# When the gMLP parameters are loaded, and into which buffers

## The chip, the cores and the metric

One core of one Trainium2 chip runs the whole block. The metric is the device time of one execution in microseconds. TensorE (PE) multiplies, VectorE (DVE) does the elementwise float work, ScalarE (ACT) copies, rounds and evaluates functions, GpSimd (POOL) helps out, and the queue of SyncE (SP) issues nearly all transfers from device memory.

## The reference, cut to what matters

The kernel computes one transformer-like layer on 512 tokens of width 1024: an adaptive norm, one wide input product, two mixers (HGRN2 and gMLP), gates, an output product and a SwiGLU network. The change is about the gMLP mixer:

```
v = gelu(zv);  v = layer_norm(v) * ln_w + ln_b
w = where(block_mask, w_s, 0)                 # 8 groups of 128 x 128
sv = einsum('gts,bnsgc->bntgc', w, v) + b_s   # over 4 blocks of 128 tokens
return gelu(zu) * sv
```

## The kernel before, in words

Every float32 operand of a large product is split in two: a high half, a rounded copy made by ScalarE ("whi", "uh", "mix"), and a low half, the remainder, made by VectorE ("wlo", "ul", "mix"). One product of 128 x 128 x 512 is then three matmuls. The split halves of the weights have two buffers each, so the split for one block can begin when TensorE is done with the block before the last.

The stage in question comes in this order on TensorE. First the last block of zu (256 columns). Then the 1024 x 1024 product zv, made with seven half-size products instead of eight (`zt7`, lines 579 to 620): seven factors in the order 1, 2, 5, 6, 7, 4, 3, of 24 matmuls each. Factors 1, 2 and 4 use quarters of the activations as they are; 5, 7, 6 and 3 use sums of quarters, made by `mixes` (lines 542 to 577): four sums "uq" of high and low halves, the difference "mixs", three further sums, and four splits into "mix". On the side of the weights, factors 5, 6, 7 and 4 use sums of two quarters of the weights, formed in place (line 191). The quarters are loaded as they come up: two into the rotating buffers "raw", two ("rawq", lines 170 to 178) into the pool ua.

After zv come the norm of gelu(zv) (`ln_fin`, `affine`), the gate product (`zw`, line 676), and between its pieces the spatial products (`spatial`, line 661), which need the transposed spatial weights "wT" and the bias "bsb".

Two pools matter. ua has twelve buffers of 8 KB per partition; at this time it holds the activations' halves uh and ul (two buffers each), and then the parameter tiles "glnp" and "bw", the six tiles of `mixes` and the two rawq. ub has five; gu takes two, gv two. A third pool has one buffer of the tag "s4", used by the staging tile "wst" of the spatial weights and by "mixs" in turn. A tile that gets a used buffer waits until the last reader of its former owner is done.

The instructions of TensorE and of the SP queue run in the order of the program. Those of VectorE, ScalarE and GpSimd are ordered beforehand by a planner, with the program's order as priority, and each engine then keeps that order. `keep_in_program_order` sets an instruction behind the one written before it on its engine. `later(n, fn)` calls fn after n ticks; a tick is half of a 128-column product, or half a factor. Four ticks pass in the last block of zu and two in each factor. `get` splits the next block one tick on, and issues the load of the block after it.

Before the change the parameters were loaded (lines 623 to 633) ahead of the last block of zu; `w_transpose` (line 635) stood between that block and `mixes`. It transposes the eight 128 x 128 matrices on TensorE into two PSUM banks, and VectorE copied them into wT, leaving out the masked corner.

Of the kernel before, what the change touches and what calls it, by code (L numbers as in the profile page):

```python
# [7 lines left out]
F32 = mybir.dt.float32  # L8
F32R = mybir.dt.float32r
U8 = mybir.dt.uint8  # L10
AF = mybir.ActivationFunctionType
OP = mybir.AluOpType
# [3 lines left out]
P = 128  # L16
T = 512
NT = T // P
D = 1024
# [12 lines left out]
def f32(ap):  # L32
    return ap.bitcast(F32)
# [17 lines left out]
def body(ctx, tc, x, c, w_ada, b_ada, w_in, b_gate, lb_logits, norm_w, w_proj_a, g_ln_w, g_ln_b,  # L51
# [3 lines left out]
    w_ada, b_ada, w_in, b_gate, norm_w = w_ada[0], b_ada[0], w_in[0], b_gate[0], norm_w[0]  # L55
    w_proj_a, g_ln_w, g_ln_b, g_ws, g_bs = w_proj_a[0], g_ln_w[0], g_ln_b[0], g_ws[0], g_bs[0]
# [3 lines left out]
    V, A, G, PE = nc.vector, nc.scalar, nc.gpsimd, nc.tensor  # L60
# [5 lines left out]
    ua = ctx.enter_context(tc.tile_pool(name="ua", bufs=12))  # L66
# [8 lines left out]
    def acc_ps():  # L75
        return acc.tile([P, 512], F32, name="acc")

    def side_ps():
        return side.tile([P, 512], F32, name="sps")

    def s2(name="s2"):
        return tmp["s2"].tile([P, 512], F32, name=name, tag="s2")

    def s4(shape, name):
        return tmp["s4"].tile(shape, F32, name=name, tag="s4")
# [6 lines left out]
    def bcast_rows(dst, src_row, n):  # L92
        nc.sync.dma_start(dst, bass.AP(tensor=src_row.tensor, offset=src_row.offset, ap=[[0, P], [1, n]]))
# [6 lines left out]
    def later(n, fn):  # L100
        queued[0] += 1
        pending.append((clock[0] + n, queued[0], fn))
# [199 lines left out]
    def ln_fin(st):  # L302
        mv = sm.tile([P, 2], F32, name="mv")
        V.bn_aggr(mv, st)
        rn = sm.tile([P, 2], F32, name="rn")
        V.tensor_scalar(rn[:, 0:1], mv[:, 1:2], LN_EPS, None, op0=OP.add)  # L306
        G.tensor_tensor(rn[:, 0:1], rn[:, 0:1], mhalf[:, 0:1], OP.pow)  # L307
        V.scalar_tensor_tensor(rn[:, 1:2], mv[:, 0:1], -1.0, rn[:, 0:1], op0=OP.mult, op1=OP.mult)
        return mv, rn

    def affine(xa, mv, rn, wb):

        V.scalar_tensor_tensor(xa, xa, mv[:, 0:1], wb[:, 0, :], op0=OP.subtract, op1=OP.mult)
        V.scalar_tensor_tensor(xa, xa, rn[:, 0:1], wb[:, 1, :], op0=OP.mult, op1=OP.add)  # L314
# [65 lines left out]
    def split_act(src, hi, lo):  # L380
        A.activation(hi, src, AF.Copy)  # L381
        V.tensor_tensor(lo, src, f32(hi), OP.subtract)  # L382
# [6 lines left out]
    ub = es_b.enter_context(tc.tile_pool(name="ub", bufs=5))  # L389
# [125 lines left out]
    gate1 = st4.tile([P, D], F32, name="gate1", tag="gate")  # L515
# [7 lines left out]
    def zw(n, evac, ah=None, al=None, j0=0):  # L523

        for j in range(j0, j0 + n, 2):
            w = get()
            for i in range(2):
                ps = acc_ps()
                gemm_w(ps, w, slice(i * P, (i + 1) * P), ah or uh, al or ul)
                evac(j + i, ps)  # L530
# [8 lines left out]
    def quarter(ap, i, j):  # L539
        return ap.u[j][:, :, i * 256:(i + 1) * 256]  # L540

    def mixes(pool, pinned=False):

        uq = {}

        def whole(i):
            t = pool.tile([P, 8, 256], F32, name="uq", tag="u")
            for j in range(2):
                uq[i, j] = t[:, 4 * j:4 * j + 4]
                ins = V.tensor_tensor(uq[i, j], f32(quarter(uh, i, j)), f32(quarter(ul, i, j)), OP.add)  # L550
                if pinned and i == 1:
                    tc.keep_in_program_order(ins)

        def part(n, src):
            t = pool.tile([P, 2, 4, 256], F32R, name="mix", tag="u")
            mix[n] = [t[:, 0], t[:, 1]]
            split_act(src, *mix[n])

        def first():
            whole(1)  # L560
            uq["s"] = s4([P, 4, 256], "mixs")
            V.tensor_tensor(uq["s"], uq[1, 0], uq[1, 1], OP.subtract)
            part(5, uq["s"])

        def second():
            whole(0)
            V.tensor_tensor(uq[1, 0], uq[0, 0], uq[1, 0], OP.subtract)
            part(7, uq[1, 0])

        def third():  # L570
            V.tensor_tensor(uq[0, 0], uq["s"], uq[0, 0], OP.subtract)
            part(6, uq[0, 0])

        def fourth():
            V.tensor_tensor(uq[0, 1], uq[0, 1], uq[0, 0], OP.add)
            part(3, uq[0, 1])
        return [first, second, third, fourth]
# [42 lines left out]
                tick()  # L620


    lnp = ua.tile([P, 2, D], F32, name="glnp", tag="u")
    bcast_rows(lnp[:, 0, :], g_ln_w, D)
    bcast_rows(lnp[:, 1, :], g_ln_b, D)
    bw = ua.tile([P, 2, D], F32, name="bw", tag="u")
    bsb = bw[:, 0, :].rearrange("p (g t) -> p g t", g=8)
    wT = bw[:, 1, :].rearrange("p (g t) -> p g t", g=8)
    bcast_rows(bw[:, 0, :], g_bs.rearrange("g t -> (g t)"), D)
    wst = s4([P, 8, P], "wst")  # L630
    nc.sync.dma_start(wst, g_ws.rearrange("g t s -> t g s"))
    V.memset(wT[64:128, :, 0:64], 0.0)
    bcast_rows(gate1, b_ada[2 * D:3 * D], D)

    def w_transpose():
        for h in range(2):
            ps = side_ps()
            for g in range(4):
                PE.transpose(ps[:, g * P:(g + 1) * P], wst[:, 4 * h + g, :], ident)
            ps = ps.rearrange("p (g t) -> p g t", g=4)  # L640
            V.tensor_copy(wT[0:64, 4 * h:4 * h + 4, :], ps[0:64])
            V.tensor_copy(wT[64:128, 4 * h:4 * h + 4, 64:128], ps[64:128, :, 64:128])

    zw(8 - NL, lambda j, ps: A.activation(gu[j], ps, AF.Gelu), j0=NL)
    w_transpose()
    for fn in mixes(ua):
        fn()
    gv = [ub.tile([P, 2, D], F32, name=f"gv{i}", tag="u") for i in range(2)]
    zt7(lambda tt: gv[tt // 2][:, tt % 2, :], AF.Gelu)
    for tt in (2, 3, 0, 1):  # L650
        va = gv[tt // 2][:, tt % 2, :]
        bst = sm.tile([P, 2, 6], F32, name="bst")
        for i in range(2):
            V.bn_stats(bst[:, i, :], va[:, i * 512:(i + 1) * 512])
        mv, rn = ln_fin(bst)
        affine(va, mv, rn, lnp)

    gmh = Big(ua, 8, F32R, "gmh", "u")
    gml = Big(ua, 8, F32R, "gml", "u")
# [1 line left out]
    def spatial(g):  # L661
        ps = side_ps()
        for n in range(NT):
            PE.matmul(ps[:, n * P:(n + 1) * P], gv[n // 2][:, n % 2, g * P:(g + 1) * P], wT[:, g, :], start=True, stop=True)  # L664
        sv = s2("sv")
        V.tensor_tensor(sv.rearrange("p (n t) -> p n t", n=NT), ps.rearrange("p (n t) -> p n t", n=NT),
                        bsb[:, g:g + 1, :].to_broadcast([P, NT, P]), OP.add)
        V.tensor_tensor(sv, sv, gu[g], OP.mult)
        split_act(sv, gmh[g], gml[g])

    for g in range(8):
        later(8 + g, lambda g=g: spatial(g))
# [23 lines left out]
    ub = es_b.enter_context(tc.tile_pool(name="ubh", bufs=1))  # L696
# [184 lines left out]
    for i in range(3 * NH):  # L881
        h = i // 3
        if i % 2 == 0:
            w = get()
        ps = acc_ps()
# [16 lines left out]
    ub = es_b.enter_context(tc.tile_pool(name="ubf", bufs=5))  # L902
# [125 lines left out]
    for tt in range(NT):  # L1028
        ht = h1t(tt)
        bst = sm.tile([P, 2, 6], F32, name="bst")  # L1030
        for hf in range(2):
            first = hf == 0 and tt < 2
            ps = head[tt] if first else acc_ps().rearrange("p (a b) -> p a b", a=2)
# [6 lines left out]
        with ahead_of_weights():  # L1040
            mv, rn = ln_fin(bst)
# [133 lines left out]
    for i, e in enumerate(order):  # L1175
# [4 lines left out]
        g, n = e  # L1180
# [48 lines left out]
    for hf in range(2):  # L1229
# [4 lines left out]
        ps = [acc_ps() for _ in range(NT)]  # L1234
# [46 lines left out]
```

## Time and profile before

| | us |
|---|---|
| median of 3 runs | 944.83 (944.23 to 945.72) |
| profiled execution | 943.97 |
| its span | 942.2 |
| TensorE busy | 901.8 (96%) |
| VectorE busy | 733.8 (78%) |
| ScalarE busy | 410.6 (44%) |
| GpSimd busy | 144.3 (15%) |

The span is the time from the first instruction to the last; the rest of the device time lies around it. Busy times of different engines overlap. An engine's idle time matters only where the engine that ends last waits for it.

### The profile page before, as it was taken

The numbers are of one execution on the slowest core, as the hardware profiler recorded it, in microseconds if no ns is written. First come the engines' busy times: TensorE is split into PE (matmuls) and PEld (weight loads), VectorE is DVE, ScalarE is ACT, GpSimd is POOL, SyncE is SP. The second block draws the span as 40 slices with busy tenths as digits, with TensorE's granted clock in tenths as the row PEclk, the third lists the DMA queues.
The fourth block names the chain that finished last, engine by engine and source line by source line (L and its number), as shares of the span: only waits on it lengthen the run. The fifth ranks groups of instructions, "written<-read, shape, count | busy, mean of one in ns | idle before, by whom it ended". The sixth has DMA issues, their size and how long they took to land.

```text
span 942.2 us, 13125 instructions
## 1 busy us (share of the span) xinstructions
PE 901.8 (96%) x5357; PEld 795.9 (84%) x5357; DVE 733.8 (78%) x1040; ACT 410.6 (44%) x538; POOL 144.3 (15%) x99
## 2 busy tenths in 40 slices
PE   5898799999999999999999999999999999999995
PEld 4677587888788888888888899899999999988884
DVE  5876896789888877878379887987888888974337
ACT  4354443423456665665423326734444445531210
POOL 2310010200000000000000011005665544000001
PEclk9999899999999999999999999999999999999998
DMA  9861244264063133222097642122244221832312
GB/s 304 283 205 37 89 134 143 93 212 134 9 171 90 49 86 90 60 77 90 7 349 242 250 135 91 45 90 90 90 130 141 90 90 45 313 135 90 112 45 89
DMA packets 107822, 118.33 MB, mean 126 GB/s; under 512 B 3617, under 2 KB 89714, under 8 KB 107762
## 3 DMA queue, kind: packets, MB, share of 16 engines
q1 hardware_dynamic: 106592, 117.45, 38.8%
q8 instruction: 42, 0.69, 0.3%
q10 hardware_dynamic: 1170, 0.05, 0.1%
q14 instruction: 18, 0.15, 0.0%
HBM read 115.39 MB, written 2.10 MB: 125 GB/s over the span
## 4 chain that ended last, share of the span: by engine, by line
PE 80%; DVE 11%; DMA 3%; ACT 2%; issue 2%; POOL 1%; POOLq 0%; SPq 0%; DVEq 0%; ACTq 0%
PE acc L1089 15%; PE acc L219 15%; PE acc L217 14%; PE acc L218 14%; PE sps L1089 7%; PE acc L599 5%; PE sps L599 2%; DVE adaacc L342 2%; POOL rn L307 1%; PE sps L814 1%; PE sps L361 1%; DMA ada<-in_w_ada_dram 1%; DVE h L314 1%; PE sps L858 1%; PE sps L664 1%
## 5 line engine op out<-in xcount | busy, mean ns | idle before, releaser
L1089 PE MATMUL acc<-left,prod 128*128 128x256 f32 x1296 | 159.6, 283 | 0.4 <-DVE left L382 0.4
L1089 PEld LDWEIGHTS acc<-left,prod 128*128 128x128 f32 x1296 | 157.2, 192 | 0.6 <-DVE left L382 0.6
L149 ACT ACTIVATE whi<-raw 128x1024 fp32r<-128x1024 f32 (+2 forms) x92 | 90.7, 1015 | 135.5 <-PE acc L219 64.8
L150 DVE TENSOR_TENSOR wlo<-raw,whi 128x1024 fp32r<-128x1024 f32 (+2 forms) x85 | 99.8, 1190 | 45.0 <-ACT whi L149 39.7
L217 PE MATMUL acc<-uh,whi 128*128 128x512 f32 x336 | 134.7, 401 | 0.0
L219 PE MATMUL acc<-uh,wlo 128*128 128x512 f32 x336 | 131.4, 391 | 1.2 <-DVE wlo L150 1.2
L218 PE MATMUL acc<-ul,whi 128*128 128x512 f32 x336 | 131.0, 390 | 0.0
L219 PEld LDWEIGHTS acc<-uh,wlo 128*128 128x128 f32 x336 | 63.1, 188 | 15.1 <-DVE wlo L150 1.6
L1089 PE MATMUL sps<-left,prod 128*128 128x256 f32 x576 | 73.4, 283 | 1.9 <-DVE prod L382 1.9
L218 PEld LDWEIGHTS acc<-ul,whi 128*128 128x128 f32 x336 | 63.3, 188 | 12.0
L217 PEld LDWEIGHTS acc<-uh,whi 128*128 128x128 f32 x336 | 63.2, 188 | 11.8
L1089 PEld LDWEIGHTS sps<-left,prod 128*128 128x128 f32 x576 | 70.8, 192 | 2.3 <-DVE prod L382 2.3
L342 DVE SCALAR_TENSOR_TENSOR adaacc<-ada,cond,adaacc 128x512 f32<-128x512 f32 x82 | 70.3, 857 | 2.3 <-DMA ada<-in_w_ada_dram 0.7
L307 POOL TENSOR_TENSOR rn<-rn,mhalf 128x1 f32<-128x1 f32 x16 | 18.5, 1158 | 348.1 <-DVE rn L306 348.1
L382 DVE TENSOR_TENSOR prod<-raw,prod 128x1024 fp32r<-128x1024 f32 x42 | 54.9, 1308 | 21.1 <-ACT prod L381 21.1
L218 PE MATMUL acc<-wlo,hs 128*128 128x512 f32 x176 | 68.5, 389 | 0.0
L217 PE MATMUL acc<-whi,hs 128*128 128x512 f32 x176 | 68.5, 389 | 0.0
L219 PE MATMUL acc<-whi,hs 128*128 128x512 f32 x176 | 68.5, 389 | 0.0
L381 ACT ACTIVATE prod<-raw 128x1024 fp32r<-128x1024 f32 x42 | 44.4, 1057 | 41.2 <-PE acc L1089 21.4
L382 DVE TENSOR_TENSOR prod<-rawu,prod 128x1024 fp32r<-128x1024 f32 x22 | 47.7, 2169 | 8.3 <-ACT prod L381 7.7
L867 POOL TENSOR_TENSOR ss<-ss,mhalf 128x4 f32<-128x4 f32 x8 | 8.1, 1014 | 268.1 <-DVE ss L866 268.1
L217 PEld LDWEIGHTS acc<-whi,hs 128*128 128x128 f32 x176 | 33.0, 188 | 6.9
(293 smaller groups left out, 1857.3 us busy)
## 6 DMA issues: line engine op xcount, KB each, us to landing
ada<-in_w_ada_dram SPq DMA_DIRECT2D x32, 512.0 KB, 9.2
raw<-in_w_in_dram SPq DMA_DIRECT2D x13, 1024.0 KB, 5.7
raw<-in_w_in_dram SPq DMA_DIRECT2D x24, 512.0 KB, 5.6
raw<-in_w_ffn_in_dram SPq DMA_DIRECT2D x11, 1024.0 KB, 5.2
rawu<-in_w_ffn_in_dram SPq DMA_DIRECT2D x11, 1024.0 KB, 7.8
raw<-in_w_ffn_out_dram SPq DMA_DIRECT2D x10, 1024.0 KB, 5.2
ada<-in_w_ada_dram SPq DMA_DIRECT2D x8, 1024.0 KB, 7.5
rawq<-in_w_in_dram SPq DMA_DIRECT2D x4, 1024.0 KB, 5.5
```

The lines of the kernel that those rows point to most:

```text
L149: A.activation(hi[:, k:k + n, :], self.raw[:, k:k + n, :], AF.Copy)
L150: eng.tensor_tensor(lo[:, k:k + n, :], self.raw[:, k:k + n, :], f32(hi[:, k:k + n, :]), OP.subtract)
L217: PE.matmul(ps, ah, bh, start=start, stop=False)
L218: PE.matmul(ps, ah, bl, start=False, stop=False)
L219: PE.matmul(ps, al, bh, start=False, stop=stop)
L307: G.tensor_tensor(rn[:, 0:1], rn[:, 0:1], mhalf[:, 0:1], OP.pow)
L314: V.scalar_tensor_tensor(xa, xa, rn[:, 0:1], wb[:, 1, :], op0=OP.mult, op1=OP.add)
L342: V.scalar_tensor_tensor(a, r, cond[:, k:k + 1], a, op0=OP.mult, op1=OP.add)
L381: A.activation(hi, src, AF.Copy)
L382: V.tensor_tensor(lo, src, f32(hi), OP.subtract)
L599: PE.matmul(o, a[:, k, s], b[:, k, :], start=n in (1, 5, 6) and k == 0 and a is ah and b is w[0], stop=n in (2, 4, 3) and k == 3 and a is ...
L1089: PE.matmul(ps[:, i, :], w[:, wi, k, cl], a[:, ai, k, :], start=first and st == (0, 0, 0, 0), stop=last and st == (1, 3, 0, 1), skip_group ...
```

## The change

The staging tile wst moves from the shared buffer to the pool ub. The parameter tiles, their four transfers and the memset become a function, called five ticks after the last block of zu, in the middle of factor 5; the transposes are called eight ticks after it, behind factor 6. The four copies into wT move from VectorE to ScalarE. `mixes` is called with `pinned`, which sets the two sums uq of its first step behind what is written before them on VectorE. The other lines only reach the tiles through a dictionary.

```diff
-    lnp = ua.tile([P, 2, D], F32, name="glnp", tag="u")
-    bcast_rows(lnp[:, 0, :], g_ln_w, D)
-    bcast_rows(lnp[:, 1, :], g_ln_b, D)
-    bw = ua.tile([P, 2, D], F32, name="bw", tag="u")
-    bsb = bw[:, 0, :].rearrange("p (g t) -> p g t", g=8)
-    wT = bw[:, 1, :].rearrange("p (g t) -> p g t", g=8)
-    bcast_rows(bw[:, 0, :], g_bs.rearrange("g t -> (g t)"), D)
-    wst = s4([P, 8, P], "wst")
+    wst = ub.tile([P, 8, P], F32, name="wst", tag="u")
     nc.sync.dma_start(wst, g_ws.rearrange("g t s -> t g s"))
-    V.memset(wT[64:128, :, 0:64], 0.0)
-    bcast_rows(gate1, b_ada[2 * D:3 * D], D)
+    gp = {}
+
+    def gmlp_params():
+        gp["lnp"] = ua.tile([P, 2, D], F32, name="glnp", tag="u")
+        bcast_rows(gp["lnp"][:, 0, :], g_ln_w, D)
+        bcast_rows(gp["lnp"][:, 1, :], g_ln_b, D)
+        bw = ua.tile([P, 2, D], F32, name="bw", tag="u")
+        gp["bsb"] = bw[:, 0, :].rearrange("p (g t) -> p g t", g=8)
+        gp["wT"] = bw[:, 1, :].rearrange("p (g t) -> p g t", g=8)
+        bcast_rows(bw[:, 0, :], g_bs.rearrange("g t -> (g t)"), D)
+        V.memset(gp["wT"][64:128, :, 0:64], 0.0)
+        bcast_rows(gate1, b_ada[2 * D:3 * D], D)
...
-            V.tensor_copy(wT[0:64, 4 * h:4 * h + 4, :], ps[0:64])
-            V.tensor_copy(wT[64:128, 4 * h:4 * h + 4, 64:128], ps[64:128, :, 64:128])
+            A.activation(gp["wT"][0:64, 4 * h:4 * h + 4, :], ps[0:64], AF.Copy)
+            A.activation(gp["wT"][64:128, 4 * h:4 * h + 4, 64:128], ps[64:128, :, 64:128], AF.Copy)
 
     zw(8 - NL, lambda j, ps: A.activation(gu[j], ps, AF.Gelu), j0=NL)
-    w_transpose()
-    for fn in mixes(ua):
+    later(5, gmlp_params)
+    later(8, w_transpose)
+    for fn in mixes(ua, True):
         fn()
```

## Rows read from the trace of the kernel before

**Rows 1.** The page: the span, and busy time of TensorE with its share.
```profile
span 942.2 us, 13125 instructions
PE 901.8 (96%) x5357; PEld 795.9 (84%) x5357; DVE 733.8 (78%) x1040; ACT 410.6 (44%) x538; POOL 144.3 (15%) x99
```
**Rows 2.** Waits of TensorE, whole span: who waited, for whom, us in total, times, longest.
```profile
PE sps L599 <- ACT whi L381: 5.8, 1, 5.8
PE acc L599 <- DVE wlo L382: 3.3, 2, 2.9
PE acc L219 <- DVE wlo L150: 1.2, 1, 1.2
```
**Rows 3.** Timeline of TensorE: start, us, what, idle before it and who ended that.
```profile
70.39 0.39 PE L217 MATMUL acc<-uh,whi 128*128 128x512 f32 x1
...
81.28 1.03 PE L639 MATMUL sps<-ident,wst 128*128 128x128 f32 x8
...
92.30 0.50 PE L599 MATMUL acc<-wlo,uh 128*128 128x512 f32 x1 [2.94 <-DVE wlo L382]
...
102.25 0.80 PE L599 MATMUL sps<-whi,mix 128*128 128x512 f32 x1 [5.76 <-ACT whi L381]
103.51 0.80 PE L599 MATMUL sps<-wlo,mix 128*128 128x512 f32 x1 [0.46 <-DVE wlo L382]
...
145.53 0.50 PE L219 MATMUL acc<-uh,wlo 128*128 128x512 f32 x1 [1.17 <-DVE wlo L150]
```
**Rows 4.** Windows: stretch, length, busy time of each engine, granted clock, DMA share, GB/s.
```profile
92.30:97.50 5.20, 4.19 (x17) 3.12 (x17) 5.20 (x5) 3.09 (x4) 0.00 (x0) 1.00 0.35 94
...
102.25:111.10 8.85, 8.39 (x24) 6.27 (x25) 8.73 (x8) 3.14 (x3) 0.00 (x0) 0.66 0.03 11
```
**Rows 5.** Chain of waits, 80 to 112 us: start, us, what.
```profile
94.55 5.25 DMA rawq<-in_w_in_dram
...
101.14 1.07 ACT whi L381
```
**Rows 6.** The SP queue: issues in order of time, and its longest wait for a mix.
```profile
57.67 0.50 SPq L93 DMA_DIRECT2D glnp<-in_gmlp_ln_w_dram  x1
...
60.28 2.95 SPq L93 DMA_DIRECT2D gate<-in_b_ada_dram  x1
68.13 0.38 SPq L178 DMA_DIRECT2D raw<-in_w_in_dram  x1
...
117.86 29.21 SPq L135 DMA_DIRECT2D raw<-in_w_in_dram  x4
...
SPq L178 <- DVE mix L382: 29.0, 2, 26.0
```
**Rows 7.** Timeline of VectorE.
```profile
58.73 0.48 DVE L632 MEMSET bw<- 64x512 f32 x1 [0.16 <-issue]
...
62.16 1.22 DVE L550 TENSOR_TENSOR uq<-uh,ul 128x1024 f32<-128x1024 f32 x1
...
72.69 2.36 DVE L382 TENSOR_TENSOR wlo<-raw,whi 128x1024 fp32r<-128x1024 f32 x2 [4.59 <-ACT whi L381]
81.91 0.68 DVE L641 COPY bw<-sps 64x512 f32<-64x512 f32 x1 [6.86 <-PE sps L639]
...
84.21 1.23 DVE L562 TENSOR_TENSOR mixs<-uq 128x1024 f32<-128x1024 f32 x1
85.35 1.22 DVE L382 TENSOR_TENSOR wlo<-raw,whi 128x1024 fp32r<-128x1024 f32 x1
...
91.03 1.22 DVE L382 TENSOR_TENSOR wlo<-raw,whi 128x1024 fp32r<-128x1024 f32 x1
...
99.82 2.36 DVE L191 TENSOR_TENSOR raw<-raw,rawq 128x1024 f32<-128x1024 f32 x2 [1.82 <-DMA rawq<-in_w_in_dram]
...
119.47 0.69 DVE L610 TENSOR_TENSOR gv<-acc,gv 128x512 f32<-128x512 f32 x1
```
**Rows 8.** Groups by line: a copy from PSUM on ScalarE; busy us, mean ns.
```profile
L603 ACT ACTIVATE gv<-acc 128x512 f32<-128x512 f32 x2 | 1.2, 598 | 2.5 <-PE acc L599 2.5
```

More of the change, by code (lines that the diff above doesn't have):

```diff
@@ L655, in body @@
         mv, rn = ln_fin(bst)
-        affine(va, mv, rn, lnp)
+        affine(va, mv, rn, gp["lnp"])
     gmh = Big(ua, 8, F32R, "gmh", "u")
@@ L663, in spatial @@
         for n in range(NT):
-            PE.matmul(ps[:, n * P:(n + 1) * P], gv[n // 2][:, n % 2, g * P:(g + 1) * P], wT[:, g, :], start=True, stop=True)
+            PE.matmul(ps[:, n * P:(n + 1) * P], gv[n // 2][:, n % 2, g * P:(g + 1) * P], gp["wT"][:, g, :], start=True, stop=True)
         sv = s2("sv")
         V.tensor_tensor(sv.rearrange("p (n t) -> p n t", n=NT), ps.rearrange("p (n t) -> p n t", n=NT),
-                        bsb[:, g:g + 1, :].to_broadcast([P, NT, P]), OP.add)
+                        gp["bsb"][:, g:g + 1, :].to_broadcast([P, NT, P]), OP.add)
         V.tensor_tensor(sv, sv, gu[g], OP.mult)
```

## The prediction

> **What bounds the kernel now.** I read the page first, then the waits of TensorE, the timelines of TensorE, VectorE and the SP queue between 57 and 157 us, and last the chain of waits between 80 and 112 us. The page shows TensorE busy for 96% of the span [rows 1]: what is to be won is in its few gaps. The list of its waits shows some that belong to the stage the diff touches, the seven factors of the gMLP product and the block after them [rows 2]; the timeline has four gaps there: 5.76 us until the high half of factor 5's weights is there, 2.94 us for the low half of factor 2's, 0.46 us for the low half of factor 5's, and 1.17 us for a low half in the gate block, at 145.53 us [rows 2, 3]. Together 10.33 us.
>
> A fifth cost is no gap. Ordinarily a matmul follows the last after 0.227 us: 48 of them lie between 70.39 and 81.28 us [rows 3]. Factor 5's 24 matmuls should take 24 x 0.227 = 5.45 us, with the gap of 0.46 us 5.91 us; they take the 8.85 us from 102.25 to 111.1, at a mean granted clock of 0.66 [rows 4]. So 2.94 us go to the half clock (1.2 GHz instead of 2.4) that the engine came back to after standing for 5.76 us. After the wait of 2.94 us, at 92.30, the clock was still 1.00 [rows 4]. All that can be won here is therefore 10.33 + 2.94 = **13.3 us**.
>
> Two owners stand behind it. The chain of waits runs back from factor 5 over ScalarE's split and the sum on VectorE to a transfer of 5.25 us into rawq, issued at 94.55 [rows 5]. The SP queue stood ready long before: its waits for a mix result come to 29.0 us in two, the longest 26.0 [rows 6], because the buffer that rawq gets was still that of a sum of the activations. And VectorE, which makes these sums, stood for 6.86 us until 81.91, waiting for the transposes of the spatial weights, then made four copies until 84.21, and only then began the difference "mixs" [rows 7]. The weight split at 91.03 that factor 2 waited for is the seventh of a row of mix operations and splits, spaced 1.14 us apart.
>
> **The change, part by part.**
>
> *The staging tile moves to the pool ub.* It shared the one buffer of "mixs"; so the difference no longer waits for the transposes. The activations' work can start when factor 1's split is done, at 72.69 + 2.36 = 75.05 us [rows 7]. ub then holds gu, wst and gv, five of five, and its next user comes after the transposes. Cost: nothing.
>
> *The pin.* Two sums that ran at 62.16 and 64.60, hidden, now stand behind factor 1's split: 2 x 1.14 = 2.28 us more on VectorE after 75.05 [rows 7]. The memset of 0.48 us moves into the crowded stretch as well.
>
> *The two parameter tiles are taken later.* Pool ua then holds uh and ul (four), six tiles of the mixes and the two rawq: twelve of twelve. Both rawq transfers can be issued behind the raw load of 68.13 [rows 6] and, at 5.25 us each, have landed before 80 us, where the first reader is some 10 us away. The stall of 5.76 us, its slow clock and the 0.46 us lose their cause.
>
> *Four parameter transfers move on the SP queue.* They are called after the first half of factor 5, behind rawq and ahead of the gate block's first load. Before, with the one for wst among them, they took the queue from 57.67 to 63.23 us, 5.6 us [rows 6]. They need two buffers, which the finished mix sums give back; by the row of operations below at about 91 us. The queue is then clear at about 97 us; the next load waited for a sum of VectorE until 117.86 [rows 6]. Their first reader, the norm's affine step, needs the results of factor 4, which ends after 81.28 + 6 x 5.45 = 114 us. Cost: nothing, unless those buffers come later (the third rival).
>
> *The transposes move behind factor 6.* Eight of them, 1.03 us on TensorE from 81.28 [rows 3], are paid there instead. Difference: nothing.
>
> *The four copies go to ScalarE.* VectorE is rid of 84.21 - 81.91 = 2.30 us [rows 7]. No such half-width copy on ScalarE is in the trace; the nearest row is a copy from PSUM of twice the partitions and the same 512 columns, 0.60 us [rows 8]. Four of these are 2.4 us as the upper end, the halves of two of them leave about 1.8 as the lower. They are ready at about 105 us, and the split queued behind them serves factor 4, about 6 us later: hidden at either end. [...]
>
> **What is late next.** VectorE, and that is why I don't forecast 13.3 us. From 75.05 it owes twelve mix operations (four sums uq, "mixs", three further sums, four low halves), and factor 2's two splits. In the order of the program, at 1.14 us each, that ends at 75.05 + 14 x 1.14 = 91.0 us, and TensorE, which starts factor 1 at 81.28, wants factor 2's last half at 81.28 + 31 x 0.227 = 88.3: a residual wait of 2.7 us. If the planner slips the splits in between, it is zero. From factor 6 on, one period of 5.45 us holds two sums and two splits (4.56 us) and, for two factors, two evacuations of about 0.6 us spacing (0.69 us each alone [rows 7]): 5.8 us, so some 0.35 us late twice, 0.7 us. In the gate block the wait of 1.17 us may stay in part: VectorE gets there earlier by 6.86 (idle) + 2.30 (copies) + 1.82 (wait for rawq [rows 7]) - 2.28 - 0.48 = 8.2 us, TensorE by 12.1 - 2.7 - 0.7 = 8.7, so that wait would not shrink by itself but grow to 1.7; VectorE's short pauses before it, though, get filled, and I put 0.6 us for it. Bounds of the residual: zero at one end; at the other 2.7 + 1.4 (twice the lateness) + 1.7 = 5.8 us. I take 2.7 + 0.7 + 0.6 = 4.0, near the upper end, since the activations' work comes first in the program.
>
> **The sum.** 13.3 - 4.0 = 9.3 us. The profiled execution took 943.97 us (span 942.2 and 1.77 around it), so 934.7; the median shown, 944.83, is 0.86 above it, so **935.5 us**. Nothing after 190 us should change: the stages behind meet the same order, earlier.
>
> **Rivals.**
>
> *Nothing is late (934.7 - 4.0 + 0.86 = 931.5).* The planner puts the splits into the gaps where VectorE waits for ScalarE's high halves. For it: before, it did so once (85.35, between two mix operations [rows 7]). Against it: that second split stood behind five mix operations.
>
> *The change doesn't do what it says: rawq is again given the buffer of a sum.* Its transfer then waits for the ninth operation, at 75.05 + 9 x 1.14 = 85.3, lands at 90.6, and sum, high half and low half (1.22 + 1.07 + 1.22 us) bring it to 94.1 where TensorE wanted it at 92.4 to 95. One or two us are lost, 937. If the planner also lets the wait grow to one that drops the clock, the 5.76 and 2.94 us stay and only 2.94 + 1.17 + 0.46 go: 4.6 us, 940.3. Against: by the count above, two of the twelve belong to no sum.
>
> *The SP queue blocks (slower).* Were one parameter tile given the buffer of a mix result that TensorE reads until the end of factor 3, at about 81.28 + 7 x 5.45 + 1.0 + 3.4 = 123.8 us, its own issues and the gate block's load would queue behind it: 123.8 + 2.95 for the last of these issues [rows 6] + 5.25 + 1.07 for the high half = 133.1, a stall of 9.3 us, with 2.9 us of slow clock behind it 12.2; the result would be 935.5 + 12.2 = 947.7. It decides once the buffer comes free later than about 113 us. Against it: before, the two tiles that waited got the two buffers freed first, by sums.
>
> **How the numbers follow.** This kernel's measurement can tell 0.2%, 1.9 us, from no change. Forecast (gain 7.5 to 11 us) 0.58; nothing late (11 to 13.3) 0.14; rawq late again (4 to 7.5) 0.17; a mishap of VectorE's order that eats all but 2 us 0.05; SP queue blocked 0.06. So faster 0.89, same 0.05, slower 0.06. The range from 931.5 to 940.5 holds the forecast and most of both neighbours.
>
> **What would show it.** Both rawq issues before 75 us on the SP queue; "mixs" on VectorE before 80 us; no wait of TensorE above 3 us between 81 and 150 us and a granted clock of 1.00 throughout. I am wrong if a wait for the weights of factor 5 stays above 5 us, if the gate block's first load is issued after 116 us, or if a new wait appears behind the ScalarE copies.

## The result, and the profile after

The changed kernel takes 935.43 us (median of 4 runs, 935.16 to 936.45), the kernel before, run beside it, 944.53: a ratio of 0.9905 with the 95% interval 0.9888 to 0.9922. Forecast were 935.5 us. The profiled execution has a span of 933.7 us where it was 942.2.

The whole difference lies in the stage that the change touches. I measure that stage from the first matmul of the last block of zu to the first of the product that follows the spatial step. This length is a sharper measure than the time of a run: the stretch ahead of it, whose work on TensorE no kernel here changes, let the stage start anywhere between 69.2 and 72.1 us in the profiles. In the kernel before it began at 70.39 us [rows 3]; the timeline of its TensorE has the end:
```profile
185.10 0.39 PE L217 MATMUL acc<-gmh,whi 128*128 128x512 f32 x1
```
114.71 us. The timeline of TensorE after, which answers to [rows 3] (start, us, what, idle before it and who ended that):
```profile
70.49 0.39 PE L217 MATMUL acc<-uh,whi 128*128 128x512 f32 x1
...
90.18 0.50 PE L599 MATMUL acc<-wlo,uh 128*128 128x512 f32 x1 [1.62 <-DVE wlo L382]
...
95.49 0.50 PE L599 MATMUL sps<-wlo,mix 128*128 128x512 f32 x1 [0.94 <-DVE wlo L382]
...
101.76 0.50 PE L599 MATMUL acc<-wlo,mix 128*128 128x512 f32 x1 [0.17 <-DVE wlo L382]
...
107.11 1.04 PE L642 MATMUL sps<-ident,wst 128*128 128x128 f32 x8
...
136.98 0.50 PE L219 MATMUL acc<-uh,wlo 128*128 128x512 f32 x1 [1.16 <-DVE wlo L150]
...
176.55 0.39 PE L217 MATMUL acc<-gmh,whi 128*128 128x512 f32 x1
```
106.06 us, 8.65 less. The wait of 5.76 us is gone; what is left are four waits for low halves, 3.89 us, all of them ended by VectorE. Factor 5 now runs from 94.16 to 101.20 us, at the full clock throughout. This window holds the end of factor 2 and most of factor 5 (window, length, busy of each engine, granted clock, DMA share, GB/s; before: [rows 4]):
```profile
92.40:98.90 6.50, 5.51 (x23) 3.93 (x22) 5.80 (x6) 3.11 (x4) 0.00 (x0) 1.00 0.41 161
```
The SP queue after, for [rows 6]: rawq is issued behind the raw load, the first parameter tile at 86.74, the second at 91.28, and the gate block's load, formerly at 117.86, at 110.91.
```profile
67.77 1.01 SPq L178 DMA_DIRECT2D rawq<-in_w_in_dram  x2
86.74 0.34 SPq L93 DMA_DIRECT2D glnp<-in_gmlp_ln_w_dram  x1
...
91.28 0.33 SPq L93 DMA_DIRECT2D bw<-in_gmlp_bs_dram  x1
...
110.91 27.61 SPq L135 DMA_DIRECT2D raw<-in_w_in_dram  x4
```
VectorE after, for [rows 7]: the pinned sums at 75.07, "mixs" at 77.45 where it was 84.21, factor 2's splits at 83.23 and 88.90, with four mix operations between them, and the sum that reads rawq at 91.17, without a wait for its transfer.
```profile
75.07 2.35 DVE L550 TENSOR_TENSOR uq<-uh,ul 128x1024 f32<-128x1024 f32 x2
77.45 1.23 DVE L562 TENSOR_TENSOR mixs<-uq 128x1024 f32<-128x1024 f32 x1
...
83.23 1.22 DVE L382 TENSOR_TENSOR wlo<-raw,whi 128x1024 fp32r<-128x1024 f32 x1
...
88.90 1.22 DVE L382 TENSOR_TENSOR wlo<-raw,whi 128x1024 fp32r<-128x1024 f32 x1
...
91.17 2.36 DVE L191 TENSOR_TENSOR raw<-raw,rawq 128x1024 f32<-128x1024 f32 x2
```

### The profile page after: what moved, and what is told of

It reads as the page before. It is cut to its first block, busy times and chain, and to the rows that moved or that the text cites. A ratio compares the mean times of both kernels' runs of the same rounds, so it can differ in the third digit from the quotient of the medians.

```text
span 933.7 us, 13131 instructions
## 1 busy us (share of the span) xinstructions
PE 899.9 (96%) x5357; PEld 794.2 (85%) x5357; DVE 731.7 (78%) x1036; ACT 412.4 (44%) x542; POOL 144.3 (15%) x99
## 4 chain that ended last, share of the span: by engine, by line
PE 81%; DVE 11%; DMA 2%; ACT 2%; issue 2%; POOL 1%; POOLq 0%; DVEq 0%; ACTq 0%; SPq 0%
PE acc L1093 15%; PE acc L219 15%; PE acc L217 15%; PE acc L218 15%; PE sps L1093 7%; PE acc L599 5%; DVE adaacc L342 2%; POOL rn L307 1%; PE sps L818 1%; PE sps L599 1%; DMA ada<-in_w_ada_dram 1%; DVE h L314 1%; PE sps L361 1%; PE sps L668 1%; PE sps L862 1%
## 5 line engine op out<-in xcount | busy, mean ns | idle before, releaser
L149 ACT ACTIVATE whi<-raw 128x1024 fp32r<-128x1024 f32 (+2 forms) x92 | 90.7, 1016 | 136.9 <-PE acc L219 64.8
```

What stands on the lines that cost most here:

```text
L149: A.activation(hi[:, k:k + n, :], self.raw[:, k:k + n, :], AF.Copy)
```

## Experiments

The lengths of the stage, each from one profiled execution, with the medians and the ratios to the kernel before on the same chip. The changed kernel's two profiles differ by 0.03 us in this length, and what lies behind the stage takes 757.0 to 757.3 us in all profiles but one (756.0 with the filled gap):

| kernel | stage us | median us | ratio (95%) |
|---|---|---|---|
| before | 114.71 | 944.53 | |
| after | 106.06 | 935.43 | 0.9905 (0.9888 to 0.9922) |
| after, run again | 106.09 | 935.89 | 0.9906 (0.9888 to 0.9924) |
| parameter tiles early | 108.06 | 937.92 | 0.9929 (0.9913 to 0.9946) |
| staging tile shared | 112.31 | 942.34 | 0.9975 (0.9964 to 0.9985) |
| copies on VectorE | 110.80 | 939.81 | 0.9951 (0.9937 to 0.9966) |
| before, gap filled | 113.87 | 942.05 | 0.9971 (0.9959 to 0.9983) |
| not pinned | 102.61 | 932.95 | 0.9881 (0.9859 to 0.9903) |
| two mix steps later | 106.41 | 935.92 | 0.9906 (0.9881 to 0.9931) |
| fourth step on GpSimd | 110.19 | 938.54 | 0.9937 (0.9918 to 0.9956) |
| norm later | 104.60 | 934.03 | 0.9891 (0.9869 to 0.9913) |
| not pinned, norm later | 101.19 | 932.21 | 0.9869 (0.9851 to 0.9888) |

**Which half of the change pays?** My theory (A) was that the head start of VectorE counts; the rival (B), that the quarters' early buffers count.

```diff
+    gmlp_params()            # at once, ahead of the last block of zu
-    later(5, gmlp_params)
```


> The changed kernel with its parameter tiles taken and loaded at once again (the staging tile stays apart, the copies on ScalarE, the transposes behind factor 6). Theory A, the head start of VectorE's mix work is what counts: the sums are done by 87 us, rawq is issued then instead of at 68 us and has landed by 92 to 97 us, about when VectorE (91.2 us in the changed kernel) comes to the sum that reads it; so 936 to 937.5 us, no wait of TensorE above 3 us, clock 1.00. Theory B, the buffers given to the quarters of weights at once are what counts: the wait for factor 5 comes back with 4 us or more and the half clock behind it, 940 us or more.

The median, 937.92, lies just above A's range, and the wait is not B's. rawq was issued at 87.41 on the SP queue and nobody waited for it: VectorE came to its first reader at 92.71. Timeline of its VectorE:
```profile
90.32 2.35 DVE L382 TENSOR_TENSOR wlo<-raw,whi 128x1024 fp32r<-128x1024 f32 x2
92.71 2.36 DVE L191 TENSOR_TENSOR raw<-raw,rawq 128x1024 f32<-128x1024 f32 x2
```
There was no wait for factor 5 at all. One for factor 2 took its place, because with other buffers the planner put both of factor 2's splits (90.32) behind all twelve mix operations; it was longer than A had allowed. Timeline of its TensorE:
```profile
91.59 0.80 PE L599 MATMUL acc<-wlo,uh 128*128 128x512 f32 x1 [3.97 <-DVE wlo L382]
```
and the window after it:
```profile
92.00:94.00 2.00, 2.00 (x6) 1.54 (x6) 1.97 (x3) 0.00 (x0) 0.00 (x0) 0.50 0.98 307
```
The half clock followed. So the tiles' later loading is worth 2.0 us of the stage, by the order that it gives VectorE, not by the transfer that it lets go earlier.

The other half alone, with the staging tile in the shared buffer:
```diff
-    wst = ub.tile([P, 8, P], F32, name="wst", tag="u")
+    wst = s4([P, 8, P], "wst")
...
-    later(8, w_transpose)
+    later(8, w_copy)         # ScalarE's four copies
+    w_transpose()            # eight transposes, left in PSUM
```


> The changed kernel with the staging tile in the shared buffer again: the eight transposes run before factor 1 and stay in PSUM until ScalarE copies them out behind factor 6, so that rawq still gets its buffers at once and VectorE makes no copies, but mixs waits for the transposes as before (82 us instead of 77.5). Theory A (head start): VectorE is 4.6 us later with all mix work, TensorE's waits for factors 2 and 5 grow from 2.6 to 6 or 7 us together; 939 to 941.5 us, with a drop of the clock in the upper half of that. Theory B (buffers): 935.4 to 936.5 us.

942.34 us: A's direction, 0.8 beyond its range; B is refuted. The wait stands in the timeline of its VectorE: 5 us idle, then "mixs" at 84.00 instead of 77.45. The idle time is booked on a high half of ScalarE, because the planner put factor 2's first split ahead of "mixs"; "mixs" could in any case not begin before the transposes, which start at 81.80 us on TensorE, had read the staging tile.
```profile
75.50 2.35 DVE L550 TENSOR_TENSOR uq<-uh,ul 128x1024 f32<-128x1024 f32 x2
82.86 1.23 DVE L382 TENSOR_TENSOR wlo<-raw,whi 128x1024 fp32r<-128x1024 f32 x1 [5.01 <-ACT whi L381]
84.00 1.22 DVE L562 TENSOR_TENSOR mixs<-uq 128x1024 f32<-128x1024 f32 x1
```
In the timeline of its TensorE factor 2 no longer waits, and factor 5 waits nearly as long as before, though rawq had been issued at 68.20 us:
```profile
99.12 0.80 PE L599 MATMUL sps<-whi,mix 128*128 128x512 f32 x1 [5.39 <-ACT whi L381]
...
101.01 0.79 PE L599 MATMUL sps<-wlo,mix 128*128 128x512 f32 x1 [1.09 <-DVE wlo L382]
```
Of the 8.65 us the head start is worth 6.25 (112.31 - 106.06). The transfer of 5.25 us on the chain of waits [rows 5] was the last to end, but VectorE, the engine that reads it, stood only 1.82 us for it in the kernel before [rows 7].

**The copies.**
```diff
-            A.activation(gp["wT"][0:64, ...], ps[0:64], AF.Copy)
+            V.tensor_copy(gp["wT"][0:64, ...], ps[0:64])
...
```


> The changed kernel with the four copies into wT on VectorE again. If VectorE is the bound of this stretch, their 2.2 us come back in part in the waits for factors 4 and 3 and of the gate block: 936 to 937.5 us. If VectorE has slack there: 935.4 us, no change.

939.81 us, and 4.74 us in the stage: the direction is that of VectorE as the bound, the size more than twice what I gave it. The copies stand in VectorE's row from 107.22 us on, and the sum for the second half of factor 4's weights comes at 111.98, where the changed kernel had it at 109.63 although its stage had begun 1.3 us later. Timeline of its VectorE:
```profile
107.22 0.68 DVE L644 COPY bw<-sps 64x512 f32<-64x512 f32 x1
...
111.98 1.22 DVE L191 TENSOR_TENSOR raw<-raw 128x1024 f32<-128x1024 f32 x1
```
Timeline of its TensorE:
```profile
114.68 0.49 PE L599 MATMUL acc<-whi,uh 128*128 128x512 f32 x1 [1.00 <-ACT whi L381]
116.13 0.50 PE L599 MATMUL acc<-wlo,uh 128*128 128x512 f32 x1 [0.95 <-DVE wlo L382]
```
and the window behind them:
```profile
118.00:120.00 2.00, 2.00 (x6) 1.56 (x5) 1.90 (x4) 0.63 (x1) 0.00 (x0) 0.50 0.99 315
```
Two new waits of 1.95 us together, one of 1.53 where it was 1.16, and matmuls at half clock for about 3.4 us, which cost about 1.7. The remaining 0.7 is in no row of the waits.

**The clock's share.** A gap filled with work tells what the half clock behind it costs.
```diff
+            if n == 5 and fn:
+                d = side_ps()
+                for _ in range(24):
+                    PE.matmul(d, uh[0][:, 0:P], uh[1], start=True, stop=True)
```


> The kernel before, with 24 matmuls whose result nobody reads (5.4 us) put ahead of factor 5, into the gap of 5.76 us; the transfer and VectorE's work are as before. If 2.9 of the 13.3 us are the half clock that follows the standstill: factor 5 runs at full clock and the time is 941.6 us. If the clock would fall anyway, or the slow matmuls have another cause: 944.5 us or more.

The median fits the first, 942.05, but the stage doesn't: it is only 0.84 us shorter. Of the 2.4 us by which the span of the profiled execution is shorter, 0.5 lie ahead of the stage and 1.1 behind it, where one of two waits for an FFN split is missing (1.1 us where the other profiles have 1.8 to 2.1), for which no run shows a reason. The clock stayed at 1.00 over factor 5; but at full speed TensorE then ran into VectorE. Timeline of its TensorE, from the 24 filling matmuls on:
```profile
95.82 5.60 PE L596 MATMUL sps<-uh 128*128 128x512 f32 x24
101.77 0.49 PE L603 MATMUL sps<-whi,mix 128*128 128x512 f32 x1 [0.35 <-ACT whi L381]
103.03 0.50 PE L603 MATMUL sps<-wlo,mix 128*128 128x512 f32 x1 [0.77 <-DVE wlo L382]
...
105.34 0.50 PE L603 MATMUL sps<-wlo,mix 128*128 128x512 f32 x1 [0.65 <-DVE wlo L382]
```
and windows over factor 5:
```profile
104.00:106.00 2.00, 1.35 (x6) 0.77 (x6) 2.00 (x3) 0.00 (x0) 0.00 (x0) 1.00 0.00 0
106.00:108.00 2.00, 2.00 (x10) 1.61 (x9) 2.00 (x3) 1.47 (x2) 0.00 (x0) 1.00 0.00 0
```
So the slow clock's 2.94 us were no loss of their own in the kernel before: about two thirds of them hid a VectorE that was late anyway.

**What is left.** Four experiments on the remaining 3.89 us. First the pin:
```diff
-    for fn in mixes(ua, True):
+    for fn in mixes(ua):
```


> The changed kernel without the pin, so that the planner may put the two first sums ahead of factor 1's split again. If the pin costs what the sum put down for it, VectorE gets 2.3 us of its crowded stretch back, the waits of 1.62 and 0.94 us shrink to under 1 us together, and the time is 933.5 to 934.5 us. If the planner then puts factor 2's second split behind all mix work, as its order of instructions shows here, that wait stays and the time is 935 to 937 us.

932.95 us and a stage of 102.61, better than either expectation: the planner moved not only the two sums (the second at 64.92) but "mixs" too ahead of factor 1's split, to 68.34, into time in which VectorE stands. Three operations at 1.14 us, 3.4 us, leave the crowded stretch, and the stage is 3.45 us shorter. Timeline of its VectorE:
```profile
64.92 1.23 DVE L550 TENSOR_TENSOR uq<-uh,ul 128x1024 f32<-128x1024 f32 x1
...
68.34 1.22 DVE L562 TENSOR_TENSOR mixs<-uq 128x1024 f32<-128x1024 f32 x1
...
87.19 1.22 DVE L382 TENSOR_TENSOR wlo<-raw,whi 128x1024 fp32r<-128x1024 f32 x1
88.33 2.36 DVE L191 TENSOR_TENSOR raw<-raw,rawq 128x1024 f32<-128x1024 f32 x2
```
Factor 2's second split does stand behind all mix operations, as the other expectation had it, but these end early enough. No wait in the seven factors is left in the timeline of its TensorE; the gate block's stays, at 1.17 us.

The steps needed last, later:
```diff
-    for fn in mixes(ua, True):
-        fn()
+    m4 = mixes(ua, True); m4[0](); m4[1]()
+    later(4, m4[2]); later(4, m4[3])
```


> The changed kernel with the third and fourth step of the mixes (four operations of VectorE, needed for factors 6 and 3 only) called four ticks later, behind the splits of factors 2 and 5 in the program. If what is left of the waits for factors 2 and 5 (2.6 us) is VectorE working in the order of the program, they vanish: 932.5 to 934 us, and no new wait above 1 us for factor 6. If VectorE's total work in the stretch is the bound, the wait only moves to factors 6 or 7: 935 to 936 us.

No gain (a stage of 106.41; the median, 935.92, is in the second expectation's range). The wait for factor 2 vanished, the one for factor 5 stayed, and longer ones for factor 6 (1.30 us where it was 0.17) and in the gate block came instead, in the timeline of its TensorE:
```profile
93.85 0.49 PE L599 MATMUL sps<-wlo,mix 128*128 128x512 f32 x1 [0.93 <-DVE wlo L382]
...
100.28 0.50 PE L599 MATMUL acc<-wlo,mix 128*128 128x512 f32 x1 [0.68 <-DVE wlo L382]
102.55 0.50 PE L599 MATMUL acc<-wlo,mix 128*128 128x512 f32 x1 [0.62 <-DVE wlo L382]
...
137.47 0.50 PE L219 MATMUL acc<-uh,wlo 128*128 128x512 f32 x1 [2.18 <-DVE wlo L150]
```
In this stretch it is VectorE's amount of work behind 75 us that binds, not its order alone.

The fourth step on GpSimd:
```diff
-            V.tensor_tensor(uq[0, 1], uq[0, 1], uq[0, 0], OP.add)
+            G.tensor_tensor(uq[0, 1], uq[0, 1], uq[0, 0], OP.add)     # and its low half
```


> The changed kernel with the fourth step of the first mixes (one sum, one low half, 2.3 us of VectorE) on GpSimd, idle in this stretch. Its sums of this size take 2.4 us there in the kernel before. If VectorE's work is the bound, the waits for factors 2 and 5 lose about 2 us: 933 to 934 us. If the two engines slow each other, or the wait has another cause: 935 us or more.

938.54 us, worse by 4.1 us in the stage: the second branch came true. The sum took 7.82 us on GpSimd, not 2.4. GpSimd's timeline:
```profile
85.07 7.82 POOL L577 TENSOR_TENSOR uq<-uq 128x1024 f32<-128x1024 f32 x1 [28.36 <-DVE uq L572]
94.06 2.35 POOL L558 TENSOR_TENSOR mix<-uq,mix 128x1024 fp32r<-128x1024 f32 x1 [1.17 <-ACT mix L557]
```
ScalarE's next high half waited for it, VectorE, done at 90.67, stood 5.91 us until GpSimd had made the low half, the splits for factor 5 stood behind that, and factor 5 waited 4.13 us with the half clock behind it. Timeline of its ScalarE:
```profile
92.93 1.06 ACT L557 ACTIVATE mix<-uq 128x1024 fp32r<-128x1024 f32 x1 [5.91 <-POOL uq L577]
...
94.84 2.00 ACT L381 ACTIVATE whi<-raw 128x1024 fp32r<-128x1024 f32 x2
```

The norm of two token tiles, behind the split of the gate's second block:
```diff
-    for tt in (2, 3, 0, 1):
-        ...
+    gnorm(2); gnorm(3)
+    later(2, lambda: (gnorm(0), gnorm(1)))
```


> The changed kernel with the norm of the first two token tiles called two ticks later, behind the split of the gate product's second block. If the wait of 1.16 us there is VectorE doing the norm first, it vanishes and the spatial products still find the norm done: 934 to 934.5 us. If VectorE is the bound up to the spatial products, a wait appears there: 935 to 936 us.

934.03 us; the wait of 1.16 us is gone, none appears at the spatial products, and the stage is 1.46 us shorter.

**Both together**, beside the changed kernel again:
```diff
-    for fn in mixes(ua, True):
+    for fn in mixes(ua):
...
+    later(2, lambda: (gnorm(0), gnorm(1)))
```


> The changed kernel without the pin and with the norm of the first two token tiles called two ticks later. Each alone took away its waits (no pin: those of factors 2 and 5; the later norm: 1.16 us in the gate product). If they are independent: no wait of TensorE between 70 and 180 us above 0.5 us, the way from the last block of zu to the first product behind the spatial step 101.4 us in place of 106.1, and about 931.5 us. If the one's gain comes out of the same slack of VectorE as the other's: a wait appears at the spatial products, 932.5 to 933.5 us.

> The changed kernel unchanged, beside the last one on the same chip: 935.4 us, as in its first runs, if the chip does not matter; the differences of the other experiments are read against it.

932.21 us against 935.89. The median lies between the two expected times; the waits and the stage are those of the first. The stage is 101.19 us, 13.52 less than before. Of TensorE's waits for a low half of the factors one is left in the whole span, 0.3 us in the second product of this kind, behind 200 us (who waited, for whom, us, times, longest):
```profile
PE acc L599 <- DVE wlo L382: 0.3, 1, 0.3
```
The two gains add up (3.45 + 1.46 of 4.87), so they are independent. This version beats both kernels.

## Why the prediction was right

- **The ceiling of 13.3 us** was nearly right as an amount, and a little too low: the last kernel takes 13.5 us out of the stage. A wait costs more than its row says: beside the wait of 1.62 us, factors 1 and 2 of the changed kernel took 12.79 us, 1.90 more than 48 matmuls at 0.227 us, and the later norm gave back 1.46 us for a wait of 1.16. As a sum of independent terms it was wrong: with the gap filled, the clock's 2.94 us shrank to 0.84. They can be had only together with an earlier VectorE.
- **The residual of 4.0 us** was 4.6 (13.3 - 8.65), 3.9 of it waits that the timeline lists. Its terms were off and made up for each other, which is luck: factor 2 waited 1.62 us instead of 2.7, since the planner let one split pass the mix work; factor 5, put down at nothing, waited 0.94; the lateness in factors 6 and 7 was 0.17 instead of 0.7; the gate block kept its whole 1.16 us instead of 0.6. That VectorE would be the next bound is shown by every one of these waits, and by the copies put back on it.
- **The owner** was named half right. The text gave the wait for factor 5 to rawq's buffer, and its gain to the early transfer; that step is wrong for the larger part, since VectorE stood only 1.82 us for the transfer [rows 7]. The runs give 6.25 of the 8.65 us to VectorE's head start, and of the 2.0 us that the tiles' later loading brings none to the transfer. These amounts are not shares of a whole: 6.25, 2.0 and the copies' 4.74 come to more than 8.65, since each is what goes when one part alone is taken back.
- **The pin** was put down at 2.28 us more on VectorE; it costs 3.45 us of the stage, since "mixs" is held back with it. Of the parts that were taken back one by one it is the only one that loses time.
- **The copies on ScalarE** were rightly put down as hidden there. They took 0.58 and 0.38 us, 1.93 for the four, between the bounds of 1.8 and 2.4, in the timeline of ScalarE after:
```profile
108.32 0.58 ACT L644 ACTIVATE bw<-sps 64x512 f32<-64x512 f32 x1
108.91 0.38 ACT L645 ACTIVATE bw<-sps 64x256 f32<-64x256 f32 x1
```
On VectorE the same two took 0.68 and 0.43. So for this float32 copy out of PSUM, VectorE was the slower of the two. The Trainium skill ("ScalarE: Activation LUTs", "Rules for kernel authors") gives VectorE up to about three times ScalarE's speed per element for single-source operations in bf16. No run here has such an operation, and the figure is no price for these copies.
- **The SP queue** went as worked out: the buffers were free at 86.7 and 91.3 us, well ahead of the 113 us from which the slower rival would have decided, and the gate block's load was issued at 110.9, ahead of the 116 that would have shown the forecast wrong. Both rawq left before 75 us, "mixs" ran before 80, no wait exceeded 3 us and the clock stayed at 1.00.

What stays open: how much of the 2.0 us for the early tiles is the planner's order and how much would remain under a fixed order; no run held the order fixed. And the run again of the changed kernel shows how far a forecast to the tenth was luck: its median is 0.46 us off its own first.

## What to carry to other kernels

A transfer that ends last on the chain of waits need not be what costs the time: ask when the engine that reads it would have come to it without the wait, and price the removal at the difference. Where an engine stands idle behind an instruction that waits in its queue, moving that instruction's cause away is worth the idle time, as far as other work can fill it; and whatever sets work behind other work there (a pin, a shared buffer) has the same price in reverse. Time lost to a half clock after a gap adds to a gain only if the engines that feed TensorE can keep up at full clock.

## What the runs showed of the hardware

A GpSimd sum of two 128 x 1024 float32 operands took 7.82 us in a stretch in which VectorE was busy until 90.7 us without a pause; in the FFN the kernel before has the same form at 2.41 and 3.39 us. VectorE's own operations beside it kept their 1.22 us. In the FFN of the kernel before, operations of VectorE beside GpSimd's sums took 2.44 and 2.83 us instead. GpSimd's long sum ended 2.2 us after VectorE had fallen idle, and its next operation of that size, beside an idle VectorE, took 2.35 us: as if it had got to work only when VectorE stopped. No run tests that.

The granted clock fell to 0.50 with one wait of 3.97 us (parameter tiles early), and also behind two waits of 1.00 and 0.95 us with one matmul between them (copies on VectorE); after single waits of 2.94 (kernel before) and 1.62 us (after) it stayed at 1.00.
